# A hybrid decoder layer on one core: a written order of two engines at a hand-over, new PSUM banks and fixed buffers for streamed slabs

## The chip, the core and the metric

The kernel runs on one core of a Trainium2 chip. The time is device microseconds of one execution, the median of several runs. The core's engines are TensorE (PE in the rows), VectorE (DVE), ScalarE (ACT), GpSimd (POOL) and SyncE (SP), whose queue issues nearly all DMAs here. SBUF is the memory on the core; PSUM holds matmul results in eight banks, numbered 0 to 7 here.

## What is computed

One layer of a decoder for 256 tokens with a model width of 2048, in float32:

```
mod = silu(c) @ w_mod + b_mod ;  sh1, sc1, g1, sh2, sc2, g2 = split(mod, 6)
h = RMSNorm_pre(x) * (1 + sc1) + sh1
oA = sliding-window attention(h) ;  oB = gated linear attention(h)
merged = sigmoid(gA) * (oA @ Wa) + sigmoid(gB) * (oB @ Wb)
x = x + g1 * RMSNorm_post(merged @ w_out)
h = RMSNorm_pre(x) * (1 + sc2) + sh2
u = conv3(h @ w_up) ;  x = x + g2 * RMSNorm_post((silu(gate) * value) @ w_down)
```

## The kernel before

**Weights.** Every weight matrix streams from HBM in slabs of 128 rows, each as two parts of 128 x 1024 float32. Exact products are put together from a high and a low part: ScalarE casts a part to fp32r (`hi`, line 292), VectorE subtracts (`lo = raw - hi`, line 293), and TensorE multiplies three times, `mm3` (lines 287 to 289: high, low, high weights), or, in the up stage, twice for each chunk of 128 (line 338). The list `parts` holds all parts in order of use. SP loads a part 4 places ahead into one of 4 buffers `raw`; `prep` makes `hi` and `lo` 3 places ahead, in 3 buffers each.

**Aux slabs.** The slabs of `w_mod` and of the bias product are not for TensorE. `aux_step` runs after each part: it lets VectorE multiply and sum the slabs that are due (`mod_proc`, line 206; `bias_proc`, line 225) and issues loads (line 238) until 2 lie ahead of what is done (4 for the first, `early`, which have a region of their own). Later slabs take turns in the two buffers of the pool `auxp` (`auxr` in the rows).

**Stages.** In time: modulation and gate weights to 200 us; attention and value projections; branch gates and branch projections of the gated linear attention (items `wGB`, `wBB`) from about 340 to 600 us, with attention's side work between; the same for attention (`wGA`, `wBA`) to 744 us; the output projection `wO` to 843 us; then two groups of up projection and down projection. In `wGB` to `wBA` (`tok_mm`) a group is a block of 512 output columns: two banks, one for each half of the tokens, filled by four items (two for `wBA`). A gate's banks are emptied by a sigmoid on ScalarE (line 828), a projection's by a product on VectorE (line 831, or 845 and 846), which merges the two. `wGB` and `wBB` take the bank pairs of `B3` in turn, so neighbouring groups share a bank; `wGA` has (1,0), `wBA` (2,4).

**Order.** TensorE and SP run in the order in which the program is written. VectorE and ScalarE run in an order that a scheduler sets when the kernel is built. `side_step` places steps of attention, normalisations and the like between the items.

**The hand-over.** The output projection holds four column banks of 512 for each token half. Its last three slabs are held back, so that the first half's banks end earlier. `evac_out` squares and sums each bank on ScalarE (line 945, into `sqj`) and scales it on VectorE (947). After the fourth it takes a root, sum on VectorE (934), power on GpSimd (935); `x1`, the new residual, on VectorE (959) with its square sums on ScalarE (961); a second root; a diagonal matrix `diag` (119). TensorE transposes `x1` with `diag` (1002, 16 chunks of 128 for a token half, four to a bank), ScalarE applies scale and shift to three chunks of four (1011), VectorE to the fourth (1017), and VectorE splits the four into the high (1019) and low (1024) parts of `h2`. Before the second half's transposes, `h2_second` runs 40 keep-warm matmuls (989) whose result nobody reads, on bank 7.

Of the kernel before, what the change touches and what calls it, by code (L numbers as in the profile page):

```python
# [9 lines left out]
F32 = mybir.dt.float32  # L10
# [7 lines left out]
P = 128  # L18
# [20 lines left out]
def block_kernel(ctx: ExitStack, tc: tile.TileContext, x, cvec, pos, idn, cst, vec, vec2, gmask,  # L39
# [9 lines left out]
    auxp = ctx.enter_context(tc.tile_pool(name="auxp", bufs=2))  # L49
# [36 lines left out]
    sqj = const.tile([P, 512], mybir.dt.bfloat16, name="sqj")  # L86
# [167 lines left out]
    def prep(it, half):  # L254
# [13 lines left out]
        else:  # L268
            hi = hip.tile([P, HW], F32R, name="hi", tag="hi")
            lo = lop.tile([P, HW], F32R, name="lo", tag="lo")  # L270
            split_to(hi[:, :w], lo[:, :w], raw)
# [413 lines left out]
    def attn_side():  # L685
# [72 lines left out]
        def ptrans(gp, t, u, sc):  # L758
            nb = t + 1
            hn = 4 // nb  # L760
            res = []
            for par in range(2):
                ps = bank(4 + par)
                for kb in range(nb):
                    for j in range(hn):
                        nc.tensor.transpose(ps[:, (kb * hn + j) * P:(kb * hn + j + 1) * P],
                                            sc[par][:, j * nb * P + kb * P:j * nb * P + (kb + 1) * P], ident)
                pT = t2k()
                nc.scalar.copy(pT, ps)
                res.append(pT)  # L770
            return res
# [16 lines left out]
        for s in range(len(units) + 2):  # L788
            if s >= 2:
                pv(*units[s - 2], pt_q.pop(0))  # L790
            if 1 <= s <= len(units):
                pt_q.append(ptrans(*units[s - 1], sc_q.pop(0)))
            if s < len(units):
                sc_q.append(scores(*units[s]))
            yield
            yield
# [71 lines left out]
    B3 = ((0, 1), (7, 0), (1, 7))  # L868
    for n in range(4):
        for u in range(8):  # L870
            if u < 4:
                blk_item(wGB, n, u, tok_mm(h_of, u, KC, B3[2 * n % 3], gb_evac(n)), side=2 if k == 1 else 1)
                if k == 3:
                    items[-1]["start"] = drain_outs
            else:
                blk_item(wBB, n, u - 4, tok_mm(ob_of, u - 4, KC, B3[(2 * n + 1) % 3], ob_evac(n)))
# [61 lines left out]
    def evac_out(t, n, ps):  # L938

        if n == 0:  # L940
# [3 lines left out]
            S["yg"] = []  # L944
        nc.scalar.activation(sqj, ps, AF.Square, accum_out=S["ss4"][:, n:n + 1])
# [3 lines left out]
        if n < 3:  # L949
            return  # L950
        rs = rstd4(S["ss4"])
        if t == 1:
            h2_act(0, 2)
            h2_hi(0, 2)
        x1, xr = S["x1"][:, t], S["xr"][:, t]
        ss = small(4, "ss4")
# [5 lines left out]
        if t == 1:  # L962
            h2_lo_(0, 2)
            h2_act(0, 3)
        rs = rstd4(ss)
        if t == 1:
            h2_hi(0, 3)
        S["dg", t] = diag_of(rs)
        if t == 1:
            h2_lo_(0, 3)  # L970
            S["prep_up"]()

    def h2_first():
# [6 lines left out]
        for n in range(2):  # L980
            h2_act(0, n)
            h2_hi(0, n)
            h2_lo_(0, n)

    def h2_second():
# [4 lines left out]
        for n in range(4):  # L990
            h2_mm(1, n)
        for n in range(4):
            h2_act(1, n)
            h2_hi(1, n)
            h2_lo_(1, n)
# [9 lines left out]
    def h2_act(t, n):  # L1005
        ht = t2k()
        S["h2t", t, n] = ht
        pt = S["h2p", t, n]
        for j in range(3):
# [4 lines left out]
    def h2_hi(t, n):  # L1014
# [4 lines left out]
        nc.vector.tensor_copy(S["h2"][0][:, 4 * n:4 * n + 4, t * P:(t + 1) * P],  # L1019
                              ht.rearrange("p (j t) -> p j t", t=P))  # L1020

    def h2_lo_(t, n):
        hv = S["h2"][0][:, 4 * n:4 * n + 4, t * P:(t + 1) * P]
# [239 lines left out]
```

## Time and profile before

| what | value |
|---|---|
| median of 3 runs | 1607.47 us (1606.06 to 1612.89) |
| the profiled execution | 1609.7 us, span 1607.7 us, mean clock 0.993 |
| TensorE busy | 1564.5 us (97%) |
| VectorE busy | 1227.0 us (76%) |
| ScalarE busy | 824.9 us (51%) |
| mean DMA rate | 251 GB/s |
| VectorE idle before an aux multiplication, for its load | 118.5 us |
| ScalarE idle before a high part, for TensorE to free a buffer | 369.1 us |

A row of a timeline gives start, duration, engine, line, operation, output and input with their size; in brackets stands how long the engine was idle before it and what ended that. Matmuls overlap, so their durations are longer than their spacing. PEclk is the granted clock of TensorE as a share of full speed.

### The profile page before, as it was taken

How to read it: one execution, taken by the hardware profiler on the slowest of the kernel's cores; microseconds unless marked ns; L12 is line 12 of the kernel's file. 1: busy time of each engine (PE TensorE's matmuls, PEld its weight loads, DVE VectorE, ACT ScalarE, POOL GpSimd, SP SyncE). 2: the span in 40 equal slices, each digit the busy share in tenths (PEclk: the TensorE clock that was granted, in tenths of full speed). 3: DMA queues.
4: the chain of work that ended last, by engine and by line, in shares of the span. 5: the costliest groups of instructions: out<-in, count | busy, mean ns of one | idle time of the engine just before them, and what ended most of it. 6: DMA issues, size and time to landing. Idle time of an engine off the chain costs nothing.

```text
span 1607.7 us, 21285 instructions
## 1 busy us (share of the span) xinstructions
PE 1564.5 (97%) x7740; PEld 1296.4 (81%) x7740; DVE 1227.0 (76%) x1870; ACT 824.9 (51%) x1216; POOL 18.1 (1%) x35
## 2 busy tenths in 40 slices
PE   8999999999999999999999999999999999999997
PEld 6878788877776778877878888888788888888886
DVE  7999989968977767877678787887555777777446
ACT  5455565554476534433356555555335555555333
POOL 0000000000000000000000000000000000000001
PEclk9999999999999999999999999999999999999999
DMA  9999987877776888988964767676765555555564
GB/s 366 383 347 410 340 273 264 285 257 257 254 256 225 275 290 297 297 277 271 359 221 136 240 223 229 234 240 232 248 223 188 178 186 187 188 186 186 194 194 136
DMA packets 154841, 403.18 MB, mean 251 GB/s; under 512 B 12720, under 2 KB 70704, under 8 KB 154480
## 3 DMA queue, kind: packets, MB, share of 16 engines
q1 hardware_dynamic: 154736, 401.82, 73.2%
q8 instruction: 61, 1.00, 0.3%
q14 instruction: 44, 0.36, 0.1%
HBM read 399.68 MB, written 2.10 MB: 250 GB/s over the span
## 4 chain that ended last, share of the span: by engine, by line
PE 62%; DMA 18%; DVE 12%; issue 5%; ACT 2%; SPq 1%; POOL 0%; DVEq 0%; POOLq 0%; ACTq 0%
PE ps L338 31%; DMA auxr<-in_wM_dram 14%; PE ps L287 10%; PE ps L289 10%; PE ps L288 10%; DVE lo L293 5%; DMA raw<-in_wO_dram 2%; DVE auxr L206 2%; ACT hi L292 1%; DMA auxr<-in_wS_dram 1%; DMA raw<-in_wS_dram 1%; DVE y L1107 0%; SPq L250 0%; PE ps L1002 0%; ACT sqj L961 0%
## 5 line engine op out<-in xcount | busy, mean ns | idle before, releaser
L292 ACT CAST hi<-raw 128x1024 fp32r<-128x1024 f32 x521 | 545.7, 1048 | 509.2 <-PE ps L289 369.1
L293 DVE TENSOR_TENSOR lo<-raw,hi 128x1024 fp32r<-128x1024 f32 x520 | 633.4, 1222 | 172.3 <-ACT hi L292 171.8
L338 PE MATMUL ps<-h,hi 128*128 128x512 f32 x1664 | 582.1, 398 | 0.3 <-DVE h L1024 0.3
L338 PE MATMUL ps<-h,lo 128*128 128x256 f32 x1664 | 450.2, 281 | 0.0
L338 PEld LDWEIGHTS ps<-h,hi 128*128 128x128 f32 x1664 | 306.5, 188 | 69.3 <-issue 1.8
L338 PEld LDWEIGHTS ps<-h,lo 128*128 128x128 f32 x1664 | 314.1, 189 | 10.2 <-DVE lo L293 0.3
L287 PE MATMUL ps<-hi,h 128*128 128x512 f32 x608 | 240.6, 396 | 7.1 <-DVE tT L831 3.8
L206 DVE SCALAR_TENSOR_TENSOR auxr<-auxr,cact 128x1024 f32<-128x1024 f32 x128 | 156.5, 1223 | 119.0 <-DMA auxr<-in_wM_dram 118.5
L288 PE MATMUL ps<-lo,h 128*128 128x512 f32 x608 | 238.0, 391 | 1.6 <-DVE lo L293 1.5
L289 PE MATMUL ps<-hi,h 128*128 128x512 f32 x608 | 237.6, 391 | 1.5 <-DVE h L293 0.8
L287 PEld LDWEIGHTS ps<-hi,h 128*128 128x128 f32 x608 | 114.5, 188 | 33.3 <-DVE tT L831 4.2
L288 PEld LDWEIGHTS ps<-lo,h 128*128 128x128 f32 x608 | 114.5, 188 | 27.4 <-DVE lo L293 3.3
L289 PEld LDWEIGHTS ps<-hi,h 128*128 128x128 f32 x608 | 114.6, 188 | 27.1 <-DVE h L293 1.2
L288 PE MATMUL ps<-lo,act_ab 128*128 128x512 f32 x256 | 99.8, 390 | 1.4 <-DVE lo L293 1.4
L287 PE MATMUL ps<-hi,act_ab 128*128 128x512 f32 x256 | 99.6, 389 | 0.0
L289 PE MATMUL ps<-hi,act_ab 128*128 128x512 f32 x256 | 99.6, 389 | 0.0
L342 ACT ACTIVATE u<-ps 128x256 f32<-128x256 f32 x88 | 33.6, 382 | 91.1 <-PE ps L338 90.8
L206 DVE SCALAR_TENSOR_TENSOR early<-early,cact 128x1024 f32<-128x1024 f32 x64 | 78.0, 1219 | 1.3 <-ACT cact L142 1.3
L343 DVE SCALAR_TENSOR_TENSOR u<-ps,u 128x256 f32<-128x256 f32 x88 | 37.2, 422 | 41.1 <-ACT u L342 41.0
L1063 ACT ACTIVATE t2k<-u,vc 128x256 f32<-128x256 f32 x88 | 52.9, 601 | 20.0 <-DVE u L343 19.8
L288 PEld LDWEIGHTS ps<-lo,act_ab 128*128 128x128 f32 x256 | 48.0, 188 | 12.3 <-DVE lo L293 2.3
L287 PEld LDWEIGHTS ps<-hi,act_ab 128*128 128x128 f32 x256 | 48.0, 188 | 10.0
(267 smaller groups left out, 1610.9 us busy)
## 6 DMA issues: line engine op xcount, KB each, us to landing
raw<-in_wU_dram SPq DMA_DIRECT2D x176, 512.0 KB, 4.3
auxr<-in_wM_dram SPq DMA_DIRECT2D x128, 512.0 KB, 5.9
raw<-in_wD_dram SPq DMA_DIRECT2D x88, 512.0 KB, 4.7
early<-in_wM_dram SPq DMA_DIRECT2D x64, 512.0 KB, 6.6
raw<-in_wS_dram SPq DMA_DIRECT2D x32, 512.0 KB, 6.2
raw<-in_wOG_dram SPq DMA_DIRECT2D x32, 512.0 KB, 7.1
auxr<-in_wS_dram SPq DMA_DIRECT2D x32, 512.0 KB, 5.6
raw<-in_wQK_dram SPq DMA_DIRECT2D x32, 512.0 KB, 5.9
```

The costliest lines, as they stand in the source:

```text
L206: nc.vector.scalar_tensor_tensor(out=raw, in0=raw, scalar=1.0, in1=cact[:, half * HW:(half + 1) * HW], op0=ALU.mult, op1=ALU.mult, accum_o ...
L287: nc.tensor.matmul(out=o, lhsT=lh, rhs=rh, start=start, stop=False)
L288: nc.tensor.matmul(out=o, lhsT=lh, rhs=rl, start=False, stop=False)
L289: nc.tensor.matmul(out=o, lhsT=ll, rhs=rh, start=False, stop=stop)
L292: nc.scalar.copy(hi_ap, src_ap)
L293: nc.vector.tensor_tensor(lo_ap, src_ap, hi_ap.bitcast(F32), op=ALU.subtract)
L338: nc.tensor.matmul(out=o, lhsT=w, rhs=m, start=c == 0 and o is ps, stop=c == nk - 1 and o is ps)
L342: nc.scalar.activation(o, ps[:, TOK:], AF.Copy, scale=scale)
L343: nc.vector.scalar_tensor_tensor(out=o, in0=ps[:, :TOK], scalar=scale, in1=o, op0=ALU.mult, op1=ALU.add)
L1063: nc.scalar.activation(z, u, AF.Identity, scale=w2, bias=vc2[:, W_CB + f:W_CB + f + 1])
```

## The change

Four things are changed.

1. **Aux buffers.** Three fixed tiles `auxb` replace the pool. All aux slabs ahead of the up stage's own (`N_PRE`) use them in turn by three, with loads up to 3 ahead; the last ones use two of them, 2 ahead. `sqj` and the up stage's buffer `u` move into the third tile.
2. **Attention.** The transposes of probabilities, before both at once on banks 4 and 5, go one at a time through bank 4, the second one side step later.
3. **Banks.** `wGB` always (0,1), `wBB` always (5,7), `wGA` (0,1), `wBA` (2,6).
4. **The hand-over.** From the last bank of the output projection on, VectorE and ScalarE run in a written order. The low part of the first up slab's second half waits until the middle of `h2`; the second token half's first chunk is made alone and first; 52 keep-warm matmuls on bank 4 stand in the place of 40 on bank 7.

```diff
-    auxp = ctx.enter_context(tc.tile_pool(name="auxp", bufs=2))
+    auxb = [const.tile([P, HW], F32, name=f"aux{i}") for i in range(3)]
+    sqj = auxb[2][:, 768:].bitcast(mybir.dt.bfloat16)
...
-            raw = auxp.tile([P, HW], F32, name="auxr", tag="auxr")
+            raw = auxb[i % (3 if i < N_PRE else 2)]
...
-    B3 = ((0, 1), (7, 0), (1, 7))
+    B2 = ((0, 1), (5, 7))
...
-                blk_item(wGA, n, u, tok_mm(h_of, u, KC, (1, 0), ga_evac(n)), side=2 if u < 2 else 1)
+                blk_item(wGA, n, u, tok_mm(h_of, u, KC, (0, 1), ga_evac(n)), side=2 if u < 2 else 1)
...
-                blk_item(wBA, n, u - 4, tok_mm(oa_of, u - 4, 8, (2, 4), oa_evac(n)))
+                blk_item(wBA, n, u - 4, tok_mm(oa_of, u - 4, 8, (2, 6), oa_evac(n)))
...
+        with tc.manual_schedule(engines={ET.DVE, ET.Activation}):
+            out_sums(3, ps)
+            up_lo = S["prep_up"]()
+            h2_act(0, 2)
+            rs = rstd4(S["ss4"])
+            out_x1(1, rs)
+            h2_act(0, 3)
+            rs = rstd4(S["ssx"])
+            h2_shift(0, 2)
+            S["dg", 1] = diag_of(rs)
+            h2_split(0, 2)
+            h2_shift(0, 3)
+            keep_warm()
+            for n in range(4):
+                h2_mm(1, n)
+            h2_act(1, 0, range(1))
+            h2_split(1, 0, range(1))
+            h2_act(1, 0, range(1, 3))
+            h2_shift(1, 0)
+            h2_split(1, 0, range(1, 4))
+            for n in range(1, 4):
+                h2_act(1, n, range(4))
+                h2_split(1, n)
+                if n == 1:
+                    up_lo()
+                if n == 2:
+                    h2_split(0, 3)
+            S["prep_up"]()()
...
-        wm = bank(7)
-        for _ in range(40):
+    def keep_warm():
+
+        wm = bank(4)
+        for _ in range(52):
...
-        while aux_loaded < min(len(aux), aux_done + (4 if aux_done < N_EARLY - 2 else 2)):
+        while aux_loaded < min(len(aux), aux_done + (4 if aux_done < N_EARLY - 2 else 3 if aux_done < N_PRE - 2 else 2)):
```

**TensorE at the start of `wGA`** (602 us in the trace). `ps0` and `ps1` are banks; `ob` is the input of the projection that ends, `h` that of the gate. Before:

```order
L289 MATMUL ps0_5108<-hi_5207,ob_3083 128x512
L287 MATMUL ps1_5279<-hi_5229,h_113 128x512
L288 MATMUL ps1_5279<-lo_5230,h_113 128x512
L289 MATMUL ps1_5279<-hi_5229,h_113 128x512
L287 MATMUL ps1_5279<-hi_5229,h_113 128x512
L288 MATMUL ps1_5279<-lo_5230,h_113 128x512
L289 MATMUL ps1_5279<-hi_5229,h_113 128x512
L287 MATMUL ps0_5280<-hi_5229,h_113 128x512
```

Now:

```order
L294 MATMUL ps7_5030<-hi_5126,ob_3052 128x512
L292 MATMUL ps0_5195<-hi_5147,h_112 128x512
L293 MATMUL ps0_5195<-lo_5148,h_112 128x512
L294 MATMUL ps0_5195<-hi_5147,h_112 128x512
L292 MATMUL ps0_5195<-hi_5147,h_112 128x512
L293 MATMUL ps0_5195<-lo_5148,h_112 128x512
L294 MATMUL ps0_5195<-hi_5147,h_112 128x512
L292 MATMUL ps1_5196<-hi_5147,h_112 128x512
```

The order of the matmuls is the same; before, the projection's last bank, 0, was written again six matmuls later, and now it is 7 and is not among the gate's.

**VectorE just ahead of that place**, up to the products that empty the projection's last banks (`tT<-ps`). `auxr`, and now `aux_102` to `aux_104`, are the aux buffers. Before:

```order
L206 SCALAR_TENSOR_TENSOR auxr,macc<-auxr,cact 128x1024
L293 TENSOR_TENSOR lo<-raw,hi 128x1024
L206 SCALAR_TENSOR_TENSOR auxr,macc<-auxr,cact 128x1024
L210 SCALAR_TENSOR_TENSOR modc<-macc,vc 128x1
L293 TENSOR_TENSOR lo<-raw,hi 128x1024
L831 TENSOR_TENSOR tT<-ps_5107,tT 128x512
L831 TENSOR_TENSOR tT<-ps_5108,tT 128x512
```

Now:

```order
L276 TENSOR_TENSOR lo<-raw,hi 128x1024 x2
L207 SCALAR_TENSOR_TENSOR aux_103,macc<-aux_103,cact 128x1024
L211 SCALAR_TENSOR_TENSOR modc<-macc,vc 128x1
L276 TENSOR_TENSOR lo<-raw,hi 128x1024
L207 SCALAR_TENSOR_TENSOR aux_104,macc<-aux_104,cact 128x1024
L276 TENSOR_TENSOR lo<-raw,hi 128x1024
L837 TENSOR_TENSOR tT<-ps_5029,tT 128x512
L837 TENSOR_TENSOR tT<-ps_5030,tT 128x512
```

The aux multiplications still stand ahead of low parts and of the products, some of them a place earlier; three buffers take turns.

**VectorE at the hand-over**, from the last scaled bank of the output projection to the diagonal matrix and on. Before:

```order
L947 TENSOR_TENSOR t2k<-ps_6456,row 128x512
L1024 TENSOR_TENSOR h_7082<-t2k,h_7082 128x4x128
L934 TENSOR_SCALAR r4j,r4m<-ss_7071 128x4
L293 TENSOR_TENSOR lo<-raw,hi 128x1024
L1017 TENSOR_SCALAR t2k<-ps_7093,acol,modc 128x128
L959 SCALAR_TENSOR_TENSOR x_6998<-t2k,r4r,xr 128x512
L1019 CAST h_7082<-t2k 128x4x128
L959 SCALAR_TENSOR_TENSOR x_6998<-t2k,r4r,xr 128x512 x3
L1024 TENSOR_TENSOR h_7082<-t2k,h_7082 128x4x128
L1017 TENSOR_SCALAR t2k<-ps_7098,acol,modc 128x128
L934 TENSOR_SCALAR r4j,r4m<-ss_7140 128x4
L1019 CAST h_7082<-t2k 128x4x128
```

Now:

```order
L992 TENSOR_TENSOR t2k<-ps_6339,row 128x512
L940 TENSOR_SCALAR r4j,r4m<-ss_6940 128x4
L1000 SCALAR_TENSOR_TENSOR x_6867<-t2k,r4r,xr 128x512 x4
L940 TENSOR_SCALAR r4j,r4m<-ss_7012 128x4
L1042 TENSOR_SCALAR t2k<-ps_6962,acol,modc 128x128
L120 TENSOR_SCALAR diag<-ident,r4r 128x128
L1050 CAST h_6951<-t2k 128x4x128
L1051 TENSOR_TENSOR h_6951<-t2k,h_6951 128x4x128
L1042 TENSOR_SCALAR t2k<-ps_6967,acol,modc 128x128
L1050 CAST h_6951<-t2k 128x128
L1051 TENSOR_TENSOR h_6951<-t2k,h_6951 128x128
```

The low part, the casts and the subtractions have left the stretch between the last bank and `diag`; behind it stands a split of a single chunk.

## Rows read from the trace of the kernel before

**Rows 1.** The page's costliest groups: count, then busy us and mean ns of one.

```profile
L293 DVE TENSOR_TENSOR lo<-raw,hi 128x1024 fp32r<-128x1024 f32 x520 | 633.4, 1222 | 172.3 <-ACT hi L292 171.8
```

**Rows 2.** Stretches: length, busy us (count) of PE, PEld, DVE, ACT, POOL, PEclk, DMA share, GB/s.

```profile
340.00:760.00 420.00, 402.11 (x1811) 318.07 (x1810) 324.53 (x533) 203.82 (x317) 2.39 (x4) 0.99 0.81 270
600.00:610.00 10.00, 7.87 (x28) 6.32 (x29) 7.73 (x11) 2.10 (x2) 0.00 (x0) 0.83 0.85 303
700.00:710.00 10.00, 8.64 (x31) 6.96 (x32) 6.60 (x10) 2.18 (x3) 0.00 (x0) 0.83 0.75 243
745.00:750.00 5.00, 4.43 (x16) 3.61 (x17) 4.00 (x6) 0.84 (x1) 0.00 (x0) 0.66 0.93 317
845.00:849.00 4.00, 3.95 (x20) 3.95 (x21) 3.88 (x9) 2.83 (x8) 1.47 (x1) 0.57 0.24 78
```

**Rows 3.** Timeline of PE: matmuls that waited for a bank.

```profile
466.75 0.50 PE L287 MATMUL ps<-hi,ob 128*128 128x512 f32 x1 [1.50 <-ACT tb L828]
...
499.11 0.50 PE L287 MATMUL ps<-hi,h 128*128 128x512 f32 x1 [1.71 <-DVE tb L831]
...
528.86 0.50 PE L287 MATMUL ps<-hi,ob 128*128 128x512 f32 x1 [1.05 <-ACT qkv L828]
...
602.13 0.50 PE L287 MATMUL ps<-hi,h 128*128 128x512 f32 x1 [3.79 <-DVE tT L831]
...
745.57 0.50 PE L287 MATMUL ps<-hi,mg 128*128 128x512 f32 x1 [1.73 <-DVE t2k L845]
```

**Rows 4.** Timeline of PE: matmuls that waited for a low part.

```profile
348.28 0.50 PE L288 MATMUL ps<-lo,h 128*128 128x512 f32 x1 [0.91 <-DVE lo L293]
...
484.45 0.50 PE L288 MATMUL ps<-lo,ob 128*128 128x512 f32 x1 [1.62 <-DVE lo L293]
...
701.36 0.50 PE L288 MATMUL ps<-lo,oa 128*128 128x512 f32 x1 [2.15 <-DVE lo L293]
```

**Rows 5.** Timeline of DVE ahead of two of these waits.

```profile
600.80 1.28 DVE L831 TENSOR_TENSOR tT<-ps,tT 128x512 f32<-128x512 f32 x2
...
698.94 1.22 DVE L206 SCALAR_TENSOR_TENSOR auxr<-auxr,cact 128x1024 f32<-128x1024 f32 x1 [2.08 <-DMA auxr<-in_wM_dram]
```

**Rows 6.** Waits, 340 to 760 us: us in total, times, longest.

```profile
ACT hi L292 <- PE ps L289: 180.1, 97, 6.3
...
DVE auxr L206 <- DMA auxr<-in_wM_dram: 67.8, 50, 3.4
```

**Rows 7.** DMA issues, 340 to 760 us: count, KB each, median us to landing.

```profile
auxr<-in_wM_dram SPq DMA_DIRECT2D x86, 512.0 KB, 5.6
```

**Rows 8.** Timeline of ACT ahead of the wait at 466.75.

```profile
464.80 1.28 ACT L828 ACT_TABLE_LOAD   x1
```

**Rows 9.** Timeline of PE at the hand-over.

```profile
842.85 0.40 PE L289 MATMUL ps<-hi,mg 128*128 128x512 f32 x1
...
845.05 5.12 PE L989 MATMUL ps<-mg 128*128 128x256 f32 x28 [1.80 <-DVE t2k L947]
...
852.65 3.84 PE L1002 MATMUL ps<-diag,x 128*128 128x128 f32 x32 [1.05 <-DVE diag L119]
...
856.78 0.47 PE L338 MATMUL ps<-h,hi 128*128 128x512 f32 x1 [0.29 <-DVE h L1024]
```

**Rows 10.** Timeline of DVE at the hand-over.

```profile
844.91 0.68 DVE L1024 TENSOR_TENSOR h<-t2k,h 128x512 fp32r<-128x512 f32 x1
...
847.92 0.42 DVE L1019 CAST h<-t2k 128x512 fp32r<-128x512 f32 x1
```

**Rows 11.** Timeline of POOL and ACT at the hand-over.

```profile
845.75 1.47 POOL L935 TENSOR_TENSOR r4r<-r4m,mhalf 128x1 f32<-128x1 f32 x1 [8.10 <-DVE r4j L934]
...
851.61 0.67 POOL L935 TENSOR_TENSOR r4r<-r4m,mhalf 128x1 f32<-128x1 f32 x1 [4.39 <-DVE r4j L934]
...
853.85 4.30 ACT L1011 ACTIVATE t2k<-ps,modc,acol 128x128 f32<-128x128 f32 x12 [2.51 <-PE ps L1002]
...
862.92 0.39 ACT L342 ACTIVATE u<-ps 128x256 f32<-128x256 f32 x1 [1.89 <-PE ps L338]
```

More of the change, by code (lines that the diff above doesn't have):

```diff
@@ L252, in load, with prep @@
             nc.sync.dma_start(out=raw[:, :w], in_=it["src"][:, half * HW:half * HW + w])
-    def prep(it, half):
+    def prep(it, half, defer=False):
         raw = it.pop(("raw", half))
@@ L270, in prep @@
             lo = lop.tile([P, HW], F32R, name="lo", tag="lo")
-            split_to(hi[:, :w], lo[:, :w], raw)
+            nc.scalar.copy(hi[:, :w], raw)
+            if defer:
+                it["w", half] = (hi, lo)
+                return lambda: nc.vector.tensor_tensor(lo[:, :w], raw, hi[:, :w].bitcast(F32), op=ALU.subtract)
+            nc.vector.tensor_tensor(lo[:, :w], raw, hi[:, :w].bitcast(F32), op=ALU.subtract)
         it["w", half] = (hi, lo)
@@ L756, in scores, with ptrans @@
             return sc
-        def ptrans(gp, t, u, sc):
+        def ptrans(gp, t, u, sc, par):
             nb = t + 1
             hn = 4 // nb
[L761 to L771, printed above, removed]
+            ps = bank(4)
+            for kb in range(nb):
+                for j in range(hn):
+                    nc.tensor.transpose(ps[:, (kb * hn + j) * P:(kb * hn + j + 1) * P],
+                                        sc[par][:, j * nb * P + kb * P:j * nb * P + (kb + 1) * P], ident)
+            pT = t2k()
+            nc.scalar.copy(pT, ps)
+            return pT
         def pv(gp, t, u, pT):
@@ L790, in attn_side @@
                 pv(*units[s - 2], pt_q.pop(0))
[L791 to L792 removed]
+            mid = 1 <= s <= len(units)
+            if mid:
+                sc = sc_q.pop(0)
+                pt_q.append([ptrans(*units[s - 1], sc, 0)])
             if s < len(units):
@@ L795, in attn_side @@
             yield
+            if mid:
+                pt_q[-1].append(ptrans(*units[s - 1], sc, 1))
             yield
@@ L871, in block_kernel @@
             if u < 4:
-                blk_item(wGB, n, u, tok_mm(h_of, u, KC, B3[2 * n % 3], gb_evac(n)), side=2 if k == 1 else 1)
+                blk_item(wGB, n, u, tok_mm(h_of, u, KC, B2[0], gb_evac(n)), side=2 if k == 1 else 1)
                 if k == 3:
@@ L944, in evac_out, with out_sums @@
             S["yg"] = []
+        if t == 0 or n < 3:
+            out_sums(n, ps)
+        if n < 3:
+            return
+        if t == 0:
+            out_x1(0, rstd4(S["ss4"]))
+            S["dg", 0] = diag_of(rstd4(S["ssx"]))
+            return
+        with tc.manual_schedule(engines={ET.DVE, ET.Activation}):
[26 more added lines that the diff above has]
+            S["prep_up"]()()
+    def out_sums(n, ps):
         nc.scalar.activation(sqj, ps, AF.Square, accum_out=S["ss4"][:, n:n + 1])
@@ L1003, in h2_mm, with h2_act @@
                              start=True, stop=True)
[L1005 to L1009, printed above, removed]
+    def h2_act(t, n, js=range(3)):
+        if js[0] == 0:
+            S["h2t", t, n] = t2k()
+        ht, pt = S["h2t", t, n], S["h2p", t, n]
+        for j in js:
             c = 4 * n + j
@@ L1061, in go @@
             w0, w1, w2 = (vc2[:, W_CW + k * 88 + f:W_CW + k * 88 + f + 1] for k in range(3))
-            u = halves(sgp.tile([P, TOK], F32, name="u", tag="sg"), ps)
+            j = (2 * gi + part) % 3
+            u = halves(auxb[2][:, j * TOK:(j + 1) * TOK], ps)
             nc.scalar.activation(z, u, AF.Identity, scale=w2, bias=vc2[:, W_CB + f:W_CB + f + 1])
@@ L1109, in evac_y2 @@
             nc.sync.dma_start(out=out[t * P:(t + 1) * P, ns], in_=y)
+    N_PRE = len(aux)
     first_g2 = n_parts[0] + 4
@@ L1115, in block_kernel @@
             w_item(wU[i], D, up_mm(i, 0, gi))
-            if grp == 0 and gi == 0:
-                items[-1]["start"] = h2_second
-                items[-1]["up0"] = True
             if grp == 1 and gi == 2:
@@ L1137, in block_kernel @@
     late = []
-    S["prep_up"] = lambda: prep(*late.pop(0)[:2])
+    S["prep_up"] = lambda: prep(*late.pop(0)[:2], defer=True)
     def aux_step(q):
@@ L1171, in block_kernel @@
             if q >= PR and it.get("wo") == KC - 1:
-                late.append(parts[q])
+                late += parts[q:q + 2] if hf == 0 else []
             else:
@@ L1176, in block_kernel @@
                 aux_step(q)
-        if q >= PR and "up0" in it and hf == 0:
-            for pt in late:
-                prep(*pt[:2])
     assert aux_done == len(aux)
```

48 lines of the change are left out of this document (13 added, 35 removed).

## The prediction

> **What bounds the kernel now.** I began with the page and its list of groups [rows 1]: a low part takes VectorE 1.22 us, and there are 520 of them, so VectorE is the engine most likely to make TensorE wait. Then I cut the span into stretches. In the stretch from 340 to 760 us (branch gates, branch projections, start of the output projection) TensorE is busy for 402.1 of 420 us [rows 2]. So the stretch can give 17.9 us at most, plus what a lowered clock costs. Third, I read the idle time before each matmul there. Two kinds of wait make most of it. Five matmuls wait for an evacuation to empty a PSUM bank [rows 3]: 1.50, 1.71, 1.05, 3.79 and 1.73, together 9.78 us. Three large ones wait for a low part [rows 4]: 0.91, 1.62, 2.15, together 4.68. Behind the waits at 602, 701 and 745 the granted clock falls, to a mean of 0.83, 0.83 and 0.66 over 10, 10 and 5 us [rows 2], which costs 0.17 x 10, 0.17 x 10 and 0.34 x 5, 1.7 us each time. Last, the hand-over from the output projection to the up projection: from the start of its last matmul at 842.85 to the first up matmul at 856.78 [rows 9] 13.9 us pass, with the keep-warm matmuls and the transposes between.
>
> **Banks.** Before, the first token half of a new group gets a free bank, but the second half one that the group before it has just filled: six matmuls later TensorE waits until that bank is emptied. Before 602 it had stopped at 598.3; VectorE emptied both banks from 600.80 on, in 1.28 us [rows 5]. With branch gates on (0,1) and projections on (5,7) or (2,6), each pair lies idle for a whole other group before it is written again, and the output projection comes to (2,6) one part later than to bank 4. Nothing new is queued behind an evacuation for it. So the waits at 499, 528, 602 and 745 go: 1.71 + 1.05 + 3.79 + 1.73 = 8.28 us, and the falls of the clock after the last two, 2 x 1.7 = 3.4 us. What is late next would be the weights. Their high parts cost no wait, since ScalarE stood waiting for TensorE for 180.1 us of the stretch before its casts [rows 6].
>
> The fifth, at 466, I count at nothing. There ScalarE loaded an activation table for 1.28 us and only then evacuated [rows 8]. In the changed order two more such loads lie round the next gate's sigmoids, between attention exponentials, and the second transposed block, which now comes a side step later, is copied only after them; its user on TensorE follows soon. The 1.50 us gained is bounded on the other side by two loads, 2.56 us. I take 1.50 lost for 1.50 gained; ends: +1.5 and -1.1.
>
> **The third aux buffer.** VectorE multiplies streamed slabs (aux) in a fixed order among its low parts. Where a slab has not landed, everything queued behind it on VectorE waits: at 698.94 it stood 2.08 us for one, and the low part behind it held TensorE for 2.15 us at 701.36 [rows 4, 5]. In the stretch it waited 67.8 us so, 50 times, at most 3.4 us [rows 6]. 86 slabs in 420 us are one per 4.9 us, and with three buffers each load is issued one slab sooner, by 4.9 us on average. That is more than the longest wait, so long as landing stays near 5.6 us [rows 7]. The queue that issues them (SP) also holds weight loads behind an aux load that waits for its buffer; they come sooner or at the same time. I take the three waits as gone, with the clock's fall after 701: 0.91 + 1.62 + 2.15 + 1.7 = 6.38 us. Bounds: nothing, if the loads only land later, and all of it.
>
> A rule speaks against this term. The Trainium skill, page "DMA: Bandwidth & Descriptors", section "Issuing engines are not separate DMA queues", has every DMA run on the same 16 engines and interleave: a third load in flight takes from the weights' loads what it gets. In this stretch the engines are busy for a share of 0.81 at 270 GB/s [rows 2], so the trace leaves room; by the rule alone the 6.38 us would shrink toward nothing and the sum to about 13.
>
> **The hand-over.** Four steps, by the rows of before. (1) VectorE takes a cast (0.42, as at 847.92) and a subtraction (0.68) of h2 and a low part out of the way of the first root [rows 10]; the last scaled block and its sum are through some 0.9 us sooner. (2) GpSimd's power for that root took 1.47 us beside VectorE's low part against 0.67 for the second one [rows 11]; the low part is deferred, and I take the 0.8 between them. (3) The cast that stood between the residual sums, at 847.92 [rows 10], goes: 0.3 us. So the transposes, at 852.65 before [rows 9], start about 850.6, 2.0 sooner. (4) After them h2's second token half is now made with its first chunk alone, so the first up matmul starts 3.8 us sooner, near 853.0. But it then outruns VectorE. From that chunk to the last four, VectorE has a shift, three chunks, four splits of some 1.0 us (cast and subtraction overlap) and the deferred low part of 1.22 us before it: 0.4 + 0.8 + 4 x 1.05 + 1.2 = 6.6 from 853.0 on, so the last four chunks come at about 859.6, and four pairs of matmuls follow. Before, sixteen pairs from 856.78 gave a result that ScalarE took at 862.92 [rows 11]; with 0.4 us for the end of the last one that is 0.36 a pair. So now the result is there at 859.6 + 4 x 0.36 + 0.4 = 861.4, a gain of 1.5 us. ScalarE, at 0.36 us a chunk (12 in 4.30 [rows 11]), is ahead of VectorE.
>
> The keep-warm matmuls must fit. 28 of them took 5.12 us at a clock that averaged 0.57 [rows 2, 9], 0.18 each, so 52 could last 9.5 us, and started at 843.1 would end at 852.6, 2 us after the transposes are ready. Now they use bank 4, free since the copies of the first token half, and follow the last projection matmul with no wait (1.80 before [rows 9]), so no fall should come; at two thirds of that time, 0.12 each, a third of a pair above, they end near 849.4. Bounds of the hand-over: 0.6 us lost to 3.8 gained.
>
> On step (2) the Trainium skill, page "SBUF — State Buffer", section "SBUF: two separate sides", says that an operation of VectorE with two SBUF inputs locks a port pair against a GpSimd operation that reads SBUF, and that the loser blocks fully. It would name the low part as the cause of the 1.47, and have the 0.8 come back in full. Only a scaling from PSUM stands beside the second root in the new order, which by the rule holds nothing.
>
> **The sum.** 8.28 + 3.4 + 6.38 + 1.5 = 19.6 us. Against the profiled execution of 1609.7 us this is 1590.1; that execution lies 2.2 above the median of 1607.47, and from the median the sum gives 1587.9. I take **1589 us**. About 0.5% of the time, 8 us, is what a measurement of this kernel can tell from no change; faster begins below 1599.5.
>
> **The rivals.** *New waits for old.* The banks are free, but attention's side work, with its table loads and its later block, and the low parts queued on VectorE hold TensorE where a bank held it before. For it: VectorE is busy for 324.5 of 420 us [rows 2], and aux operations moved one place ahead in its order at many places. Against: each of the waits named ended with its own evacuation, and TensorE did not wait at the next matmul. Half of the 18.1 us of banks and aux terms, 9, then stays: with 1.5 from the hand-over about 1598. *The third buffer brings nothing*: loads land later by as much as they start sooner, since the DMA engines are the limit. Then 8.28 + 3.4 + 1.5 = 13.2, or about 1595. The rule of the Trainium skill on the 16 shared engines leads here. Against: slices of the stretch reach 303 and 317 GB/s where its mean is 270 [rows 2]. *The change doesn't do what it says*: the bank waits are only the last of several waits that end together; gain under 4 us, 1604 to 1609. Against: 3.79 us is longer than any other wait near it. *Slower.* Aux operations now stand before low parts, and if landing grows beyond 5.6 + 4.9 = 10.5 us, each late slab holds TensorE as at 701: 2.15 + 1.7 = 3.85 us. To come out over 1615.5 it must eat the 13.2 us of the other terms and 8 more, 5.5 such stalls beyond the three of before; ten would give about 1633. Nothing in the rows puts landing there.
>
> **How the numbers follow.** Forecast 0.66; new waits 0.16; third buffer brings nothing 0.09; no effect 0.05; slower 0.04. The forecast case itself spans its unknowns: up by 1.5 at 466 and 2.3 more at the hand-over, and the smaller waits that I left (about 3 us in the stretch) give 1581; down by 1.1, 2.0 and a part of the aux term give 1596. The 8 in 10 needs the third-buffer case, inside that, and the near half of the new waits: **1581 to 1600**. Faster by over 0.5%: 0.66 + 0.09 + more than half of the 0.16, 0.85. Within: the rest of it, 0.05 and a little of the slower, 0.12. Slower 0.03.
>
> **What would show it.** In the trace of the changed kernel the first matmuls of each half of a branch gate's or projection's group have no wait for VectorE or ScalarE; the clock of the slices at 600, 700 and 745 us is 1.00; VectorE's wait for aux in the stretch falls from 67.8 us to under 20; landing stays below 8 us. At the hand-over GpSimd's first power takes near 0.6 us, the transposes come 7.8 us after the start of the last projection matmul where it was 9.8, and the first up matmul 10 us after it where it was 13.9, then with several short waits for VectorE. I am wrong if TensorE's idle time in the stretch stays above 10 us: then the waits named were not the last ones, or landing has grown.

## The result and the profile after

The changed kernel took 1597.11 us, the median of its runs, against 1606.65 us for the kernel before beside it. Five of its six runs lie between 1590.40 and 1597.75 us, with a median of 1596.48; the sixth was a slow one of 3146.69 us, which the ratio leaves out and the median does not. The ratio is 0.9934, with a 95% interval of 0.9915 to 0.9954: about 10 us less, where 19.6 were forecast. The time lies in the upper part of the range of 1581 to 1600. Differences below are taken from 1597.11; from 1596.48 each would shift by 0.6 us. The profiled execution took 1597.75 us, its span is 1595.6 us, and the mean clock rose from 0.993 to 0.997.

The page of the changed kernel has TensorE busy for 98% of the span, 97% before. Its group of aux multiplications (busy us, mean ns, then idle us before them and what ended it):

```profile
L207 DVE SCALAR_TENSOR_TENSOR aux<-aux,cact 128x1024 f32<-128x1024 f32 x128 | 156.4, 1223 | 145.7 <-DMA aux<-in_wM_dram 145.6
```

This line is the surprise: VectorE stands 145.7 us before its aux multiplications, where it was 118.5 us before. The forecast had this wait fall: in the stretch from 340 to 760 us from 67.8 to under 20 us.

Stretches of the changed kernel, columns as in [rows 2]:

```profile
340.00:760.00 420.00, 411.38 (x1864) 325.32 (x1863) 331.48 (x544) 209.81 (x321) 2.39 (x4) 1.00 0.83 280
470.00:475.00 5.00, 4.12 (x14) 1.96 (x14) 4.33 (x6) 4.54 (x7) 0.00 (x0) 0.66 0.17 46
600.00:610.00 10.00, 10.00 (x46) 8.14 (x45) 8.43 (x13) 3.68 (x4) 0.00 (x0) 1.00 0.98 343
```

From 340 to 760 us TensorE is busy for 411.4 of 420 us, 402.1 before: of 17.9 us of idle time 8.6 are left, where the waits that the sum takes away (8.28 + 4.68) would have left 4.9. The clock at 600 us is 1.00, where it was 0.83; at 700 and 745 us it is 1.00 too. A new fall, to 0.66, stands at 470 us and costs 0.34 x 5 = 1.7 us.

The timeline of TensorE in the same stretch, the larger of its waits:

```profile
470.88 1.71 PE L783 MATMUL ps<-t2k,qkv 128*64 128x512 f32 x2 [2.38 <-ACT t2k L772]
...
685.26 0.50 PE L293 MATMUL ps<-lo,h 128*128 128x512 f32 x1 [1.36 <-DVE lo L276]
...
739.60 0.50 PE L292 MATMUL ps<-hi,mg 128*128 128x512 f32 x1 [0.77 <-DVE mg L298]
```

None of the five bank waits of [rows 3] is left. Of the three low-part waits of [rows 4], 348 us still has 0.53; the others are gone, but new ones stand elsewhere, the largest 1.36 at 685 us. And at 470.88 TensorE waits 2.38 us for a copy of attention's transposed block.

The starts of the same matmuls in both timelines show where the lead comes and goes:

| first matmul of | before, us | after, us | lead, us |
|---|---|---|---|
| first branch projection `wBB` | 412.18 | 410.98 | 1.2 |
| third block of gates `wGB` | 495.88 | 495.33 | 0.6 |
| `wGA`, first block | 596.42 | 593.73 | 2.7 |
| its projection `wBA` | 624.27 | 615.65 | 8.6 |
| third `wBA` | 693.39 | 688.39 | 5.0 |
| output projection | 742.80 | 732.97 | 9.8 |
| its last slab | 835.37 | 821.40 | 14.0 |
| up projection | 856.78 | 839.69 | 17.1 |
| first down projection | 1105.59 | 1091.64 | 14.0 |
| second up group | 1227.34 | 1215.30 | 12.0 |

The wait of 3.79 us with its fall of the clock is the step from 2.7 to 8.6. The low-part wait of 2.15 at 701 with its fall is most of that from 5.0 to 9.8. New waits take 3.6 us back before 693, and the up and down stages another 5.1 behind the hand-over, a part of it in the first up slab, which starts early and then waits.

### The profile page after: what moved, and what is told of

Same layout as the page of the kernel before. It is cut to its first block, busy times and chain, and to the rows that moved or that the text cites. A ratio compares the mean times of both kernels' runs of the same rounds, so it can differ in the third digit from the quotient of the medians.

```text
span 1595.6 us, 21287 instructions
## 1 busy us (share of the span) xinstructions
PE 1563.3 (98%) x7752; PEld 1293.2 (81%) x7752; DVE 1222.5 (77%) x1869; ACT 825.7 (52%) x1221; POOL 17.0 (1%) x35
## 4 chain that ended last, share of the span: by engine, by line
PE 31%; DMA 22%; DVE 13%; issue 5%; ACT 2%; SPq 1%; POOL 0%; DVEq 0%; POOLq 0%; ACTq 0%
DMA aux<-in_wM_dram 21%; PE ps L343 16%; DVE lo L276 6%; PE ps L293 5%; PE ps L294 5%; PE ps L292 5%; DVE aux L207 2%; DMA raw<-in_wO_dram 1%; ACT hi L272 1%; SPq L251 0%; DVE aux L348 0%; DVE t2k L742 0%; DVE t2k L1093 0%; DVE y L1134 0%; SPq L253 0%
## 5 line engine op out<-in xcount | busy, mean ns | idle before, releaser
L207 DVE SCALAR_TENSOR_TENSOR aux<-aux,cact 128x1024 f32<-128x1024 f32 x128 | 156.4, 1223 | 145.7 <-DMA aux<-in_wM_dram 145.6
L347 ACT ACTIVATE aux<-ps 128x256 f32<-128x256 f32 x88 | 33.5, 380 | 75.4 <-PE ps L343 75.2
L1090 ACT ACTIVATE t2k<-aux,vc 128x256 f32<-128x256 f32 x88 | 52.8, 601 | 26.6 <-DVE aux L348 26.4
L348 DVE SCALAR_TENSOR_TENSOR aux<-ps,aux 128x256 f32<-128x256 f32 x88 | 37.0, 421 | 35.6 <-ACT aux L347 35.6
```

The source lines that it names most:

```text
L207: nc.vector.scalar_tensor_tensor(out=raw, in0=raw, scalar=1.0, in1=cact[:, half * HW:(half + 1) * HW], op0=ALU.mult, op1=ALU.mult, accum_o ...
L347: nc.scalar.activation(o, ps[:, TOK:], AF.Copy, scale=scale)
L348: nc.vector.scalar_tensor_tensor(out=o, in0=ps[:, :TOK], scalar=scale, in1=o, op0=ALU.mult, op1=ALU.add)
L1090: nc.scalar.activation(z, u, AF.Identity, scale=w2, bias=vc2[:, W_CB + f:W_CB + f + 1])
```

## Experiments

**Which part brought what, in the scheduler's order.** Three kernels each undo one part of the change.

Two aux buffers instead of three:

```diff
-            raw = auxb[i % (3 if i < N_PRE else 2)]
+            raw = auxb[i % 2]
...
-(4 if aux_done < N_EARLY - 2 else 3 if aux_done < N_PRE - 2 else 2)
+(4 if aux_done < N_EARLY - 2 else 2)
```

> The changed kernel with two aux buffers again, loads up to 2 ahead; all else as changed. Theory A (the queue order): in the changed kernel SP waits only 1.9 us for aux buffers from 340 to 760 us but 201 us for weight buffers that VectorE's low parts free, so the third buffer is hardly ever what an aux load waits for, and VectorE's wait for aux did not fall (67.8 before, 77.7 after). Without it the time stays within 3 us of the changed kernel's (1597). Theory B, the prediction's term: the third buffer brought up to 6.4 us, so the time rises to about 1603. VectorE's wait for aux in the stretch: A 65 to 85 us, B over 90.

It took 1604.79 us (ratio to before 0.9995, 0.9977 to 1.0013), 7.7 more than the changed kernel. Theory A missed the time, theory B VectorE's wait: it is theory A's. The waits of this kernel from 340 to 760 us, first VectorE's and TensorE's (us in total, times, longest), then SP's:

```profile
DVE aux L207 <- DMA aux<-in_wM_dram: 77.0, 57, 4.0
...
PE ps L293 <- DVE lo L276: 9.2, 13, 2.1
```

```profile
SPq L239 <- DVE aux L207: 24.4, 17, 4.0
```

The same waits in the changed kernel:

```profile
DVE aux L207 <- DMA aux<-in_wM_dram: 77.7, 58, 4.2
...
PE ps L293 <- DVE lo L276: 4.8, 7, 1.4
```

```profile
SPq L251 <- DVE lo L276: 201.3, 76, 9.7
...
SPq L239 <- DVE aux L207: 1.9, 2, 1.0
```

And SP's in the kernel before:

```profile
SPq L250 <- DVE lo L293: 186.5, 74, 8.8
...
SPq L238 <- DVE auxr L206: 27.5, 18, 4.2
```

VectorE waits 77 us for aux in both; over the whole execution it waits 113.6 us with two buffers and 145.6 with three, and the kernel with two is the slower, so the sum of these waits does not give the time. But with two buffers SP stands 24.4 us at aux buffers, with three 1.9, and TensorE's waits for low parts are 9.2 us against 4.8. It seems that the third buffer freed SP's queue, not VectorE: a weight load behind a blocked aux load comes sooner. That this is the way from the one to the other was not tested apart, and the order of VectorE differs between the two kernels as well, as shown further down.

The banks and the attention transposes of before:

```diff
-    B2 = ((0, 1), (5, 7))
+    B3 = ((0, 1), (7, 0), (1, 7))
...
-            ps = bank(4)
+            ps = bank(4 + par)
```

> The changed kernel with the PSUM banks of before (gates and projections in turn over 0, 1 and 7, then (1,0) and (2,4)) and both transposes of attention at once on banks 4 and 5; aux buffers and hand-over as changed. Theory A: the bank waits are most of the gain. They come back near 499, 528, 602 and 745 us, 6 to 8 us, with falls of the clock of 1.7 us behind the two longest, while the new wait of 2.4 us at 471 us with its fall of about 1.7 us goes: 1602 to 1605. Theory B (the waits were only the last of several): within 2 us of 1597.

It took 1602.60 us (0.9978, 0.9959 to 0.9997; runs from 1597.32 to 1609.74), 5.5 more. Theory A, at the lower edge of its numbers, and the interval only just clears the changed kernel's. The 5.5 are a net figure: bank waits of 1.05, 1.91, 2.51, 2.92 and 1.60 us are back, and the wait of 2.38 us at 471 with its fall of the clock is gone.

The hand-over of before, with the rest as changed:

```diff
-        with tc.manual_schedule(engines={ET.DVE, ET.Activation}):
...
-            keep_warm()
+                items[-1]["start"] = h2_second
```

> The kernel before with the new banks, attention steps and aux buffers, but the hand-over as before: scheduler's order, 40 keep-warm matmuls on bank 7. Theory A: the hand-over alone gave 1.2 us until the first up slab's end (18.9 against 20.1 us from the last projection matmul to the copy of its result), so 1598 to 1600. Theory B: the written order also cost about 1.7 us in the up stage behind it (244.4 against 242.7 us from that copy to the first down matmul), so undoing it costs nothing: 1595 to 1598.

1595.85 us (0.9942, 0.9924 to 0.9959): not to be told from the changed kernel, as theory B said. In the profiled executions the time from the start of the output projection to that of the first down projection is 358.6 us here and 358.7 there. Runs of these kernels scatter by 7 us and more (1593.1 to 1600.7 here), so 1 us can't be read.

**What VectorE waits for.** The changed kernel's SP timeline and, below it, VectorE's at the same place:

```profile
562.89 0.51 SPq L239 DMA_DIRECT2D aux<-in_wM_dram  x1
563.61 4.88 SPq L251 DMA_DIRECT2D raw<-in_wBB_dram  x2
568.53 0.50 SPq L239 DMA_DIRECT2D aux<-in_wM_dram  x1
...
565.46 1.22 DVE L207 SCALAR_TENSOR_TENSOR aux<-aux,cact 128x1024 f32<-128x1024 f32 x1 [1.88 <-DMA aux<-in_wM_dram]
...
566.87 1.22 DVE L276 TENSOR_TENSOR lo<-raw,hi 128x1024 fp32r<-128x1024 f32 x1
568.95 1.22 DVE L207 SCALAR_TENSOR_TENSOR aux<-aux,cact 128x1024 f32<-128x1024 f32 x1 [0.86 <-DMA aux<-in_wM_dram]
...
573.50 1.23 DVE L207 SCALAR_TENSOR_TENSOR aux<-aux,cact 128x1024 f32<-128x1024 f32 x1 [1.04 <-DMA aux<-in_wM_dram]
```

The aux load issued at 562.89 ends VectorE's wait at 568.95, 6.1 us later; the one issued at 568.53 ends that at 573.50. So this load goes out one aux multiplication ahead of its use, not three. Between the two aux loads SP issues two weight loads over 4.88 us: the second waits for a buffer that the low part at 566.87 has to free, and on VectorE that low part stands behind the aux multiplication at 565.46, which had waited 1.88 us for its own load.

Pairing each aux load of SP's timeline from 340 to 760 us with its use on VectorE gives the same for the whole stretch:

| kernel | aux loads | with 0, 1, 2 aux multiplications started between issue and use | mean us from issue to use | median landing, us |
|---|---|---|---|---|
| before | 86 | 16, 70, 0 | 6.42 | 5.6 |
| changed | 91 | 13, 70, 8 | 6.76 | 5.7 |

The forecast had the distance from issue to use grow by 4.9 us; it grew by 0.3. The low parts that stand ahead of each aux multiplication on VectorE, counted in the traces, show what the scheduler did with the third buffer: of the 88 aux multiplications in the stretch 56 stand one to four low parts earlier than in the kernel with two buffers and the rest as changed, 25 stand at the same place and 7 later.

The next kernel, called the held kernel from here on, takes that back. An order edge queues each aux multiplication behind the low part of the part before its own place:

```diff
...
-            aux_proc(aux_done)
+            with tc.issue_after(lo_ins[-1 - 1]) if aux_done >= N_EARLY and aux_done < len(aux) else nullcontext():
+                aux_proc(aux_done)
```

> The changed kernel with one thing more: on VectorE each aux multiplication is queued behind the low part of the part before its own place in the program (an order edge, no wait), where the scheduler had put it earlier. Two more aux multiplications then always lie between the point where an aux load can be issued and its use, where it was mostly one. Theory A: VectorE's wait for aux in the stretch falls from 77.7 to under 25 us; the waits of TensorE for low parts (about 5 us there) and the wait of 2.4 us at 471 us, whose reciprocals stood behind an aux slab for 3.3 us, go with their fall of the clock: 1588 to 1592. Theory B: landing grows with more loads in flight, or the later aux work delays low parts: 1596 or more.

It took 1576.89 us (0.9828, 0.9813 to 0.9843), 20 less than the changed kernel and 29 less than before; run again beside its variants it took 1576.82. That is more than theory A said, which counted the stretch alone: in the profiled executions the held kernel leads by 12.6 us at the start of the output projection, by 15.2 at the up projection, by 16.8 at the first down projection and by 20.8 at the second up group, so 8 us come behind the stretch. Its aux multiplications, its stretch from 340 to 760 us, SP's waits there and the landing:

```profile
L207 DVE SCALAR_TENSOR_TENSOR aux<-aux,cact 128x1024 f32<-128x1024 f32 x128 | 155.9, 1219 | 0.0
```

```profile
340.00:760.00 420.00, 418.80 (x1929) 337.85 (x1928) 345.13 (x557) 212.94 (x326) 2.39 (x4) 1.00 0.88 293
```

```profile
SPq L251 <- DVE lo L278: 148.1, 80, 5.9
SPq L239 <- DVE aux L207: 67.3, 59, 4.2
```

```profile
aux<-in_wM_dram SPq DMA_DIRECT2D x94, 512.0 KB, 5.9
```

VectorE's idle time before aux is 0.0 us, and TensorE is busy for 418.8 of 420 us. From issue to use an aux load now has 12.2 us on average, and 92 of 94 have two aux multiplications between. SP now waits for aux buffers (67.3 us) and less for low parts (148.1 for 201.3). Landing is 5.9 us, so more loads in flight at 293 GB/s made it hardly longer. The runs lie within 2.6 us, where five of the changed kernel lie within 7.4, so parts of 2 to 3 us can now be read; one of 1 us hardly.

> The kernel before with the order edge alone: each aux multiplication on VectorE behind the low part of the part before its own place; two aux buffers, banks and hand-over as before. Theory A (the time lay in VectorE standing at aux slabs that had not landed): the edge alone brings most of its 20 us here too, 1586 to 1592, and the bank waits near 466, 499, 528, 602 and 745 us stay, shorter where VectorE itself was late (602: under 2 us instead of 3.79). Theory B (the edge needs the third buffer and the new banks): over 1598.

The kernel before with the edge alone took 1587.65 us (0.9889, 0.9870 to 0.9909): theory A. Of its waits of TensorE, those for a bank:

```profile
463.57 0.50 PE L289 MATMUL ps<-hi,ob 128*128 128x512 f32 x1 [1.05 <-ACT tb L830]
...
523.39 0.80 PE L289 MATMUL ps<-hi,ob 128*128 128x512 f32 x1 [2.66 <-ACT qkv L830]
...
728.52 0.50 PE L289 MATMUL ps<-hi,mg 128*128 128x512 f32 x1 [0.20 <-DVE t2k L847]
```

The waits of 499 and 602 us are gone though the banks are as before, and that of 745 has shrunk to 0.20 at 728.52. The two behind ScalarE (1.50 and 1.05 in [rows 3]) are still there with 1.05 and 2.66. From here to the held kernel it is 10.8 us: that is what the whole change is worth once the edge is there.

> The held kernel (1576.9 us: the changed kernel with the order edge) with two aux buffers, loads up to 2 ahead. One aux multiplication instead of two then lies between the point where a load can be issued and its use: 4.9 us on average against a landing of 5.7. Theory A (with the edge, the third buffer is what covers the landing): VectorE waits for aux again, 40 to 70 us in the stretch from 340 to 760, and SP more for buffers; 1581 to 1587. Theory B (the edge alone is enough): 1576 to 1579.

The held kernel with two aux buffers took 1579.86 us, 3.0 more. VectorE's wait for aux in its stretch:

```profile
DVE aux L207 <- DMA aux<-in_wM_dram: 13.1, 14, 2.0
```

13.1 us: less than theory A's 40 to 70, and the time lies between the two theories' numbers. The edge does most, the third buffer the rest. Of the 3.0 us about half can't be laid to the buffer: in the profiled execution 1.5 us are lost before 200 us, where the clock fell to 0.83 from 110 to 120 us and in the held kernel did not (below, at the keep-warm matmuls).

> The held kernel (1576.9 us) with the banks and attention transposes of before. Theory A (bank waits cost what the rows of before said, 8 to 10 us with the falls of the clock): 1584 to 1587. Theory B (a part of these waits was VectorE coming late to the evacuation because it stood at an aux slab, as at 602 us): about half, 1580 to 1583, with no single wait over 2 us.

With the old banks it took 1584.96 us (1582.03 to 1585.22), 8.1 more; in its profiled execution of 1582.03:

```profile
462.02 0.50 PE L294 MATMUL ps<-hi,ob 128*128 128x512 f32 x1 [1.05 <-ACT tb L834]
...
521.84 0.50 PE L294 MATMUL ps<-hi,ob 128*128 128x512 f32 x1 [2.66 <-ACT qkv L834]
...
725.38 0.50 PE L294 MATMUL ps<-hi,mg 128*128 128x512 f32 x1 [0.20 <-DVE t2k L851]
```

The waits are theory B's, with one of 2.66 us over its bound of 2; the time is theory A's in the median. The waits that are left sum to 3.9 us and are in line with the 5.1 us of the profiled execution. That was the fastest run, with a mean clock of 0.998; the three others, 1584.70 to 1585.22, had 0.995 or 0.996, which over 1580 us is 3 to 5 us. So what they lose besides is clock; where, no trace shows.

Whether the clock falls behind a wait differs from one execution to another. The same wait of 2.66 us stands at 523 us in the kernel before with the edge alone and at 522 us here. The stretch behind it there, with the granted clock at 0.82:

```profile
525.00:530.00 5.00, 5.00 (x24) 3.65 (x22) 3.39 (x4) 1.66 (x2) 0.00 (x0) 0.82 0.50 168
```

and here, at 1.00:

```profile
525.00:530.00 5.00, 5.00 (x31) 3.67 (x30) 4.66 (x7) 2.47 (x4) 0.00 (x0) 1.00 0.77 228
```

> The held kernel (1576.9 us) with the hand-over as before: scheduler's order, 40 keep-warm matmuls on bank 7. Theory A (the written order gains 1.2 us to the first slab's end and loses nothing behind it): 1578.1. Theory B (it gains nothing, as the run with the old hand-over and the changed rest said, 1595.9 against 1597.1): 1575 to 1577.

With the old hand-over it took 1578.29 us (1577.47 to 1579.21, against 1576.60 to 1579.17), 1.4 more: in the direction of theory A, though the runs overlap. In the profiled executions it is 19.7 us from the last projection matmul to the copy of the first slab, 18.9 in the held kernel.

**The hand-over, further.** The changed kernel's own, timelines of TensorE, GpSimd and ScalarE:

```profile
828.33 0.40 PE L294 MATMUL ps<-hi,mg 128*128 128x512 f32 x1
...
836.12 3.81 PE L1027 MATMUL ps<-diag,x 128*128 128x128 f32 x32 [1.18 <-DVE diag L120]
839.69 0.48 PE L343 MATMUL ps<-h,hi 128*128 128x512 f32 x1
...
843.48 0.47 PE L343 MATMUL ps<-h,hi 128*128 128x512 f32 x1 [0.61 <-DVE h L1051]
...
845.51 0.50 PE L343 MATMUL ps<-h,hi 128*128 128x512 f32 x1 [0.41 <-DVE h L1051]
...
830.41 0.55 POOL L941 TENSOR_TENSOR r4r<-r4m,mhalf 128x1 f32<-128x1 f32 x1 [7.28 <-DVE r4j L940]
...
847.23 0.39 ACT L347 ACTIVATE aux<-ps 128x256 f32<-128x256 f32 x1 [2.71 <-PE ps L343]
```

The transposes start 7.8 us after the last projection matmul, as forecast, and GpSimd takes 0.55 us. But the first up matmul comes 3.6 us after the transposes' start, since all 32 of them (3.81 us) stand before it on TensorE; the sum had 2.4 (850.6 to 853.0). Then TensorE waits 0.61 and 0.41 us for VectorE, and the slab's result is taken 18.9 us after the last projection matmul, against 862.92 - 842.85 = 20.1 before [rows 9, 11].

Two kernels on the held one move VectorE's steps into its idle time. First the deferred low part, then also a split:

```diff
             out_x1(1, rs)
+            up_lo()
             h2_act(0, 3)
...
             h2_shift(0, 3)
+            h2_split(0, 3)
             keep_warm()
...
-                if n == 1:
-                    up_lo()
-                if n == 2:
-                    h2_split(0, 3)
```

> The held kernel with the deferred low part of the first up slab's second half placed right behind the residual sums, where VectorE stood idle for 1.13 us waiting for ScalarE's square sums, instead of between the splits of h2. Theory A (the first up slab waits for VectorE, 0.61 and 0.41 us and what it takes to start again): the last chunks come 1.1 us sooner, both waits shrink to under 0.2 in sum, and the time falls by about 1 us, to 1576. Theory B (the slab is bound elsewhere): no change, and the transposes start later by up to 0.2 us.

> As the run before, and the split of the first token half's last four chunks also ahead of the second half's first chunk, in the 0.4 us that VectorE stands idle there. Theory A: no wait of TensorE for VectorE is left in the first up slab, which ends 16 x 0.36 us after the transposes: 1.4 to 1.6 us less than the held kernel, 1575.5. Theory B: the first chunk, 0.6 us later, now holds the first up matmul, and the gain of the run before is lost again.

They took 1576.62 and 1575.69 us beside 1576.82 for the held kernel. By the medians the first is not to be told from it, though its slab was copied 0.9 us sooner in the profile; the second is 1.1 less, in the direction of theory A and short of its numbers, and its slowest run lies among those of the held kernel. Among the runs at a mean clock of 0.998 alone, the held kernel took 1576.64 to 1576.91, the first variant 1575.82 and 1575.97, the second 1575.17 to 1575.76. Held kernel, then the second variant (last projection matmul, an early up matmul in the second, the copy of the first slab):

```profile
812.94 0.40 PE L296 MATMUL ps<-hi,mg 128*128 128x512 f32 x1
...
831.84 0.39 ACT L349 ACTIVATE aux<-ps 128x256 f32<-128x256 f32 x1 [2.73 <-PE ps L345]
```

```profile
812.33 0.40 PE L296 MATMUL ps<-hi,mg 128*128 128x512 f32 x1
...
824.57 0.50 PE L345 MATMUL ps<-h,hi 128*128 128x512 f32 x1 [0.28 <-DVE h L1051]
...
830.18 0.38 ACT L349 ACTIVATE aux<-ps 128x256 f32<-128x256 f32 x1 [1.65 <-PE ps L345]
```

From the last projection matmul to the copy it is 18.9 and 17.9 us, 18.0 in the first variant. TensorE now waits 0.28 us behind the first up matmuls: a little of theory B. The second variant has the lowest median of the study, 0.9788 of before (0.9768 to 0.9809); the held kernel beside it has 0.9796.

> The held kernel once more, unchanged, beside its variants on one chip: 1576 to 1578.

The held kernel without keep-warm matmuls (`-            keep_warm()`):

> The held kernel without its 52 keep-warm matmuls (their result is read by nobody). TensorE is then idle for some 7.5 us before the second transposes. Theory A (they keep the granted clock up): the clock falls to half at the transposes or behind them for a few us, as behind the idle times of 2 to 4 us in the kernel before; transposes and first pairs take longer, 1.5 to 3 us more in all, 1578 to 1580. Theory B (the transposes don't suffer and VectorE holds the first slab anyway): within 0.7 us.

1579.66 us, 2.8 more: theory A in kind. Its transposes, and the stretches around them:

```profile
821.87 6.39 PE L1028 MATMUL ps<-diag,x 128*128 128x128 f32 x32 [7.30 <-DVE diag L120]
```

```profile
820.00:825.00 5.00, 3.13 (x14) 3.13 (x15) 2.62 (x9) 2.73 (x8) 0.55 (x1) 0.50 0.00 0
825.00:830.00 5.00, 5.00 (x31) 4.77 (x30) 4.25 (x9) 4.25 (x13) 0.00 (x0) 0.77 0.00 0
```

After 7.30 us of idle time the granted clock is 0.50 and then 0.77, and 32 transposes take 6.39 us in the place of 3.8. But not all of the 2.8 us is theirs. From the last projection matmul to the copy of the first slab it is 20.3 us, 1.4 more than in the held kernel; another 1.3 us were lost before 200 us, where the two programs do not differ. The clock from 110 to 120 us, in the held kernel and then in this one:

```profile
110.00:120.00 10.00, 9.56 (x42) 7.93 (x43) 9.96 (x20) 3.92 (x6) 0.00 (x0) 1.00 0.99 320
```

```profile
110.00:120.00 10.00, 9.82 (x36) 8.01 (x37) 9.96 (x18) 4.10 (x7) 0.00 (x0) 0.83 1.00 326
```

In both TensorE had waited 1.07 us at 109 and 0.81 us at 110 us. Three of the fourteen profiled executions of this study show this fall: this one, the held kernel with two aux buffers and the kernel before with the edge alone.

## Why the prediction was right in its direction and half right in its size

*Banks* (8.28 us, and 3.4 of clock). All four waits went, and the falls of the clock behind them. Undoing the banks and the attention steps costs 8.1 us with the edge and 5.5 in the scheduler's order, not 11.7. In the 5.5 the new wait at 471 is set off, 2.38 and 1.7 of clock; the banks alone then come to about 9.6, an estimate. The step that failed is taking a bank wait for the bank's alone. With the edge and the old banks the waits at 499 and 602 us go as well and that at 745 shrinks to 0.20. VectorE came late to the evacuation because it stood at aux slabs, as the trace of before shows ahead of 602:

```profile
594.47 1.23 DVE L206 SCALAR_TENSOR_TENSOR auxr<-auxr,cact 128x1024 f32<-128x1024 f32 x1 [2.20 <-DMA auxr<-in_wM_dram]
...
598.26 1.23 DVE L206 SCALAR_TENSOR_TENSOR auxr<-auxr,cact 128x1024 f32<-128x1024 f32 x1 [1.41 <-DMA auxr<-in_wM_dram]
```

It had also waited 1.94 us at 496 and 2.53 us at 738. So two terms of the sum had one cause in part, and the new banks or the edge, either of them, end these waits. The clock was a second weak step: the sum takes a fall behind a wait as certain, and the same wait of 2.66 us was followed by one in one execution and by none in another.

*The fifth bank wait* (0 us, ends +1.5 and -1.1). It came out below its bound: 1.50 went, 2.38 came, and 1.7 of clock with it. The place was right, the cause only in part. The timelines of VectorE and ScalarE ahead of the wait at 470.88:

```profile
467.04 1.22 DVE L207 SCALAR_TENSOR_TENSOR aux<-aux,cact 128x1024 f32<-128x1024 f32 x1 [3.30 <-DMA aux<-in_wM_dram]
...
468.66 1.70 ACT L760 ACTIVATE t2k<-t2k,dn 128x256 f32<-128x256 f32 x4 [1.50 <-DVE dn L757]
470.27 0.56 ACT L772 COPY t2k<-ps 128x512 f32<-128x512 f32 x1
```

An aux slab, 3.30 us late, held the reciprocals for ScalarE's scaling and the copy. ScalarE stood idle for 1.50 us at that place; the rest of the 2.38 is its own work ahead of the copy, two sigmoids with table loads of 1.28 us among it. In the held kernel this wait is gone.

*The third buffer* (6.38 us). Undoing it costs 7.7 us in the scheduler's order and 3.0 in the held one. That 7.7 lies near 6.38 is luck, for the way was wrong. The step that failed is "each load is issued one slab sooner". The aux load stands in SP's queue behind a weight load, which waits for a low part, which stands behind aux multiplications that the scheduler moved ahead; from issue to use the mean went from 6.42 to 6.76 us. VectorE's wait for aux was to fall under 20 us and rose from 67.8 to 77.7. The prediction had the queue the other way round only, weight loads behind aux loads. The rows were there: SP's waits in the kernel before, 186.5 us for low parts and 27.5 for aux buffers.

*The hand-over* (1.5 us). 1.4 by undoing it in the held kernel, with runs that overlap; nothing to be seen in the scheduler's order. Within it, the start of the transposes is as forecast and the first up matmul is 1.2 us later, as the transposes fill TensorE; VectorE then bounds the slab as said.

*What the sum left out.* TensorE's waits for low parts in the up and down stages, where two buffers stay: 0.39, 0.32, 0.87, 0.76 and 0.42 us in the changed kernel, 0.46 and 0.97 before; in the held one none of over 0.2 us is left behind the first slab. And a gain: the waits of 0.62, 0.77 and 0.21 us at 825 to 829 us in the kernel before are gone; with two buffers 0.76 and 0.36 are back.

*The rivals.* The outcome is nearest to "new waits for old" (about 1598). "The third buffer brings nothing" had the time, 1595, but not the mechanism: landing went from 5.6 to 5.7 us:

```profile
aux<-in_wM_dram SPq DMA_DIRECT2D x91, 512.0 KB, 5.7
```

So the rule on the 16 shared DMA engines (the Trainium skill, "DMA: Bandwidth & Descriptors", section "Issuing engines are not separate DMA queues") did not decide here. The rule on the shared port (the Trainium skill, "SBUF — State Buffer", section "SBUF: two separate sides") agrees with the row: without a low part beside it GpSimd's power takes 0.55 us for 1.47, and the second one, beside the scaling from PSUM, 0.55 too. No run changes this alone.

*The whole.* With the edge the change is worth 10.8 us, without it about 10; its three parts, undone one at a time with the edge, come to 3.0 + 8.1 + 1.4 = 12.5.

*Open.* Why undoing the third buffer costs 7.7 us in the one order and 3.0, or half of that, in the other; and what makes runs of the kernels that wait for landings scatter by 7 us: the clock alone does not, for the five runs of the changed kernel all have a mean of 0.996 or 0.997.

## What to carry over

Before a deeper buffer, read what the load really waits for: its own buffer, or what stands ahead of it in its queue. A scheduler that orders by its own model may spend the new slack on running the consumer sooner, so the wait stays; an edge that holds the consumer back can be worth more than the buffer. And of a wait for an engine, ask what that engine waited for just before: several waits may be one.

## What the hardware showed besides

With 7.3 us of idle time TensorE's clock stood at 0.50 over 5 us; the 52 keep-warm matmuls that fill this time are worth 1.4 us by the profiled hand-over, 2.8 by the medians. A fall of the clock behind a short wait is not certain: behind the same waits of 1.07 and 0.81 us near 110 us it fell in three of fourteen profiled executions. DMA engines carried 293 GB/s at a share of 0.88 over 420 us with a landing of 5.9 us, hardly more than the 5.6 us at 270 GB/s.
